# Remainders of streamed weights in a two-layer encoder trunk: an accumulating DMA onto the negated rounded part in place of a subtraction on VectorE

## Chip, cores and metric

One core of one Trainium2 chip runs the whole program. The metric is the device time of one execution in microseconds (us): 2113.9 us is the median of three runs before the change (2113.85 to 2116.01).

## The reference

The program computes a two-layer encoder trunk in float32 for one sequence of 512 tokens and 1024 features. Each layer has a SwiGLU feed-forward at half weight, a mixer, a second feed-forward, each followed by a layer norm over a scaled residual, and a gated per-layer embedding. Cut to its frame:

```python
def swiglu(x, wg, wu, wd):
    return (jax.nn.silu(x @ wg) * (x @ wu)) @ wd

def reference(x, p, ...):
    for i in range(DEPTH):
        x = layer_norm(DN_ALPHA * x + 0.5 * swiglu(x, ffn1_wg[i], ffn1_wu[i], ffn1_wd[i]), ...)
        y = mixer_ab(x, ...) if i % 2 == 0 else mixer_c(x, ...)
        x = layer_norm(DN_ALPHA * x + y, ...)
        x = layer_norm(DN_ALPHA * x + 0.5 * swiglu(x, ffn2_wg[i], ffn2_wu[i], ffn2_wd[i]), ...)
        x = x + jax.nn.sigmoid(x @ ple_wg[i] + ple_bg[i]) * (p[i] @ ple_wp[i])
    return x
```

The mixer of layer 0 is sliding-window attention beside a gated linear recurrence (mixer A and B), that of layer 1 a gated delta rule with eight heads (mixer C). The feed-forward width is 2816, so the four feed-forwards hold most of the weights.

## The kernel before

Activations lie with features on the partitions and the 512 tokens along the free axis. The weights are cut into 2776 tiles of 128x128, which the host packs in the order of their use; each tile is read from memory once.

**Products.** A float32 product is made of three passes in a rounded format (float32r). Both operands are split into a rounded part (hi) and the exact remainder (lo), and `mm3` (L338) issues lo x hi, hi x hi and hi x lo into one sum. The pass with the remainder of the weights comes first.

**The weight stream.** `dma_unit` (L293) loads a unit of eight tiles (512 KB) on SP's DMA queue into one of three buffers called wr. `splitter` (L299) splits the units by halves: a half unit is four tiles, 128x512 elements, and feeds twelve products. It allocates two tiles of the big pool (the t tiles, 93 buffers). ScalarE copies the half unit into hi with rounding, VectorE subtracts hi from the half unit and writes lo (L314 and L315):

```python
yield self.S.l.copy(hi[:, c].bitcast(F32R), r[:, c])
yield self.V.l.tensor_tensor(lo[:, c].bitcast(F32R), r[:, c], hi[:, c], ALU.subtract)
```

There are 694 half units. `splitter` runs ahead of the products by `self.ahead` half units: 4 in a feed-forward, 10 towards the end of a feed-forward or a mixer, 6 otherwise.

**The order of the work.** The program is written out by hand for each engine; each engine executes its instructions in that order and waits on semaphores. The main stream is TensorE's. All else is in chains (generators), and between two products `tick` (L233) lets each chain go on as far as its operands are there by a rough clock which the program keeps for every engine while it is built. The rough clock decides only the order.

**A feed-forward** (`ffn`, L401): eleven groups of four sums (two gate and two up tiles), each group eight half units of weights, 96 products. After a group ScalarE and VectorE read the sums from PSUM, and ScalarE goes on with the next splits. Then come the products with the third matrix, one sum after the other (`resid_ln`, L424). A feed-forward has 132 half units.

**The tail of a block** (`resid_ln`, L424, `tail`, L498): the sums of a layer norm are taken tile by tile. For the middle tiles POOL adds the values and their squares (8 to 12 additions of 128x512), for the last ones VectorE does it, and all of them build up the same two tiles; TensorE then sums over the partitions by products with a tile of ones (o), and the next block's inputs follow from that. In the two mixers three output tiles are made by halves of the tokens.

All compute instructions are issued by the helper `issue` at L100, so the profile puts nearly all of them on that line.

Of the kernel before, what the change touches and what calls it, by code (L numbers as in the profile page):

```python
"""Two-layer hybrid encoder trunk (macaron SwiGLU, sliding-window attention + RG-LRU,
gated DeltaNet, per-layer embeddings) on one NeuronCore.

Activations are feature-major ([feature on partitions, 512 tokens free]); every weight
matrix is streamed once, packed by the host in the order of its use, 128x128 tile by tile.
A float32 product is carried by three float32r passes: both operands are split exactly
into a rounded part and its remainder.
The delta rule runs in blocks of 128 tokens: v_new = beta * T (v - e^gc (k S)) with
T = (I + (strict kk^T decay) diag(beta))^-1, built by recursive block doubling.
"""  # L10
# [8 lines left out]
F32R = mybir.dt.float32r  # L19
AF = mybir.ActivationFunctionType  # L20
ALU = mybir.AluOpType
AX = mybir.AxisListType

P = 128
T = 512
# [17 lines left out]
# columns of the packed per-partition vectors  # L43
# [14 lines left out]
# columns of the constant table: identity, ones, cumulative-sum triangle, causal mask,  # L58
# compact identity, masks of the block-doubling levels
# [16 lines left out]
def cells(ap):  # L76
    """the 128-element columns of its tile that an access touches"""
    name = ap.tensor.name
    dims = list(ap.ap)
    c0 = ap.offset % dims[0][0]  # L80
    c1 = c0 + sum((n - 1) * st for st, n in dims[1:])
    return [(name, c) for c in range(c0 // P, c1 // P + 1)]


class Eng:
    """Issues to an engine and keeps a rough clock of it, by which the order of issue of
    independent work is chosen. eng.f(...) issues, eng.l.f(...) makes an Op to be issued later."""
# [25 lines left out]
    def at(self, op):  # L113
        """when the operands are there"""
        ready = self.k.ready
        return max([ready.get(c, 0.0) for x in op.ins for c in cells(x)] + [0.0])
# [44 lines left out]
class Kern:  # L161
# [44 lines left out]
    def bank(self, keep=2):  # L206
        """for chains: a PSUM bank, when more than keep are left for the main stream"""
        while len(self.banks) <= keep:
            yield None
        return self.take_bank()  # L210
# [9 lines left out]
    # The main stream is the tensor engine's, slot by slot. Chains are generators of Ops (or lists  # L220
    # of Ops of one engine); between the main stream's products each chain goes on as far as its
    # operands are there by the rough clock. None: look again later.
# [10 lines left out]
    def tick(self, share=None):  # L233
        """share: the time that chains may take on the tensor engine now"""
        if self.ticking:
            return False
        if share is not None:
            self.share = min(self.share + share, MAXSHARE)
        self.ticking = True
        moved = False  # L240
        for g in list(self.gens):
            n = 0
            while n < 12:
                n += 1
                op = g[1]
                if op is not None:
                    ops = op if isinstance(op, list) else [op]
                    if self.due_at(op) > self.PE.t or share is not None and ops[0].eng is self.PE and self.share <= 0.0:
                        break
                    t = self.PE.t  # L250
                    for o in ops:
                        o.eng.issue(o)
                    self.share -= self.PE.t - t
                    moved = True
                try:
                    g[1] = next(g[0])
                except StopIteration:
                    self.gens.remove(g)
                    moved = True
                    break  # L260
                if g[1] is None:
                    break
        self.ticking = False
        return moved
# [9 lines left out]
    def until(self, cond):  # L274
        """hold the main stream until the chains have issued what it needs"""
        n = 0
        while not cond():
            if not self.tick():
                at = [self.due_at(g[1]) for g in self.gens if g[1] is not None]
                self.PE.t = max(self.PE.t + 0.02, min(at) if at else 0.0)  # L280
            n += 1
            assert n < 100000

    def settle(self, *aps):
        """chains go on while the main stream's next operands are not there"""
        at = max([self.ready.get(c, 0.0) for x in aps for c in cells(x)] + [0.0])
        while at > self.PE.t + 0.05:
            if not self.tick():
                nxt = [self.due_at(g[1]) for g in self.gens if g[1] is not None]
                self.PE.t = max(self.PE.t + 0.02, min([at] + nxt))  # L290

# [7 lines left out]
    def splitter(self):  # L299
        """splits the weights some half units ahead of their use"""  # L300
        while self.nsplit < 2 * NUNITS:
# [9 lines left out]
            for c0, c1 in FIRST if v == 0 else ((0, HSLOT),):  # L311
                if c1 <= HSLOT:
                    c = slice(c0 * P, c1 * P)
                    yield self.S.l.copy(hi[:, c].bitcast(F32R), r[:, c])  # L314
                    yield self.V.l.tensor_tensor(lo[:, c].bitcast(F32R), r[:, c], hi[:, c], ALU.subtract)  # L315
                    self.units[v] = (hi, lo)
            self.nsplit += 1

    def w(self, desc):
        """the next weight tile of the stream, as its two parts"""  # L320
        u, s = divmod(self.nslot, HSLOT)
        if s == 0:
            # the splitter goes first when it is late
# [31 lines left out]
    def split(self, src, eng=None):  # L355
        """hi = rounded src, lo = src - hi; src in SBUF or PSUM"""
# [8 lines left out]
    def group(self, descs, x, nk=KD, halves=False):  # L365
        """the m tiles of a group advance together over k; with halves, tokens 0-255 first"""
# [20 lines left out]
    def x(self, k, cs):  # L387
        """layer input k, once its normalisation is issued"""
        half = 0 if cs.stop == T // 2 else 1
        self.until(lambda: self.napply[half] > k)  # L390
        return self.xh[k], self.xl[k]
# [32 lines left out]
    def resid_ln(self, i, l, fac, desc, y, nk, ngroup, nhalf):  # L424
        """x = LN(alpha x + fac y); y comes as 8 PSUM tiles: the first ngroup advance together
        over k, the last nhalf are made by halves of the tokens, so that the normalisation of the
        first half runs under the products of the second. Sums are taken about the mean of the
        first 128 features."""
# [55 lines left out]
        for half, cs in enumerate(HALVES):  # L484
            for m in ms:
                # a bank is not written while it is read
# [67 lines left out]
    def ple_p(self, i, ms):  # L554
        """products of p, made where the main stream would wait for a normalisation"""
# [13 lines left out]
    def ple(self, i):  # L569
# [26 lines left out]
        if last:  # L596
            # the last one by halves of the tokens, each on its way out under the other
# [19 lines left out]
    def softplus(self, x, n):  # L617
        """max(x,0) + log1p(exp(-|x|)), log1p by 2 atanh(e/(2+e))"""
# [74 lines left out]
    def attn(self, j, hh, q):  # L693
        """one head, two pairs of 128-query blocks; keys of the block and of the one before"""
# [59 lines left out]
    def conv(self, p_, cols, bias=None):  # L754
        """causal depthwise convolution over the free axis, taps w[0..3] per partition"""
# [24 lines left out]
    def rg_lru(self, t, x, pa, px):  # L780
        """with Th = tanh(-log_a / 2): y = 1/(1 + Th) by a Newton step from (1 + a)/2,
        a = 1 - 2 Th y, sqrt(1 - a^2) = 2 sqrt(Th) y"""
# [115 lines left out]
    def gdn(self, h):  # L898
# [9 lines left out]
        # decay: dt[j, i] = exp(gc_i - gc_j), j <= i  # L908
# [3 lines left out]
        # token-major k, q (for the norms) and v  # L912
# [37 lines left out]
        # U = (I + N)^-1, 32x32 diagonal blocks first (compact), then 64 and 128  # L950
# [15 lines left out]
        # level s: with the 2s blocks [lo | hi], the product of U11 N12 with U22 makes U12; two  # L966
        # chunks share a pass, the hi (then the lo) columns of both being 32
# [52 lines left out]
        # scan over the blocks  # L1020
# [149 lines left out]
# tiles of the pool; delta-rule chains at a time; heads by which a gate z follows its q, k, v  # L1170
# [3 lines left out]
# products of p made before the second feed-forward, and before the gates  # L1174
NP1, NP2 = 5, 8
# half units split ahead at the end of a feed-forward, of a mixer
AHEADF, AHEADO = 10, 10
# chains on the tensor engine: lateness allowed for operands, time per main product, bursts
PELAG, SHARE, MAXSHARE = 0.15, 0.25, 0.2
LOOK = 2  # L1180
AB_ORDER = (("bx", 1), ("q", 1), ("g", 0), ("bx", 2), ("q", 2), ("g", 1), ("bx", 3), ("q", 3), ("g", 2),
# [3 lines left out]
def c_order():  # L1185
    """the q, k, v of a head ahead of the gate z of an earlier one"""
# [26 lines left out]
def alibi():  # L1213
    """[head, query, own | previous | own keys], relative to a block of 128 queries"""
# [83 lines left out]
```

## Time and profile before

| | before |
|---|---|
| median of 3 runs | 2113.9 us (2113.85 to 2116.01) |
| span of the profiled execution | 2113.2 us |
| TensorE (PE) busy | 2093.3 us, 99% |
| TensorE weight loads (PEld) busy | 1757.3 us, 83% |
| VectorE (DVE) busy | 1102.8 us, 52% |
| ScalarE (ACT) busy | 867.1 us, 41% |
| GpSimd (POOL) busy | 145.5 us, 7% |
| DMA | 194.38 MB, mean 92 GB/s |
| mean granted TensorE clock | 0.998 |

The profiled execution is another one than the timed runs. Its own time is its span, 2113.2 us from the first to the last instruction; the runs' times hold 0.7 us more at the median. Busy shares are means over stages which differ: the four feed-forwards, the two mixers and the layer norms between them. TensorE's bounds stand out at once; where it does wait, and for whom, is in the views by time. Matmul ends are modelled, so the sum of busy time alone does not show a stall.

### The profile page before, as it was taken

Reading aid. Unit: us, or ns where it says so; the run is one execution under the profiler, and the core shown is the slowest. Engines: PE = TensorE matmul, PEld = TensorE weight load, DVE = VectorE, ACT = ScalarE, POOL = GpSimd, SP = SyncE. Lnnn points to the kernel's source line nnn. Section 1 sums busy time; section 2 is a strip of 40 time slices with the busy share of each in tenths; the row PEclk is TensorE's granted clock in tenths of the full one; section 3 lists DMA queues with packets and bytes.
Section 4 is the critical chain, followed back from the end, with each engine's and each line's share of the span. In section 5 each row is a group of like instructions: output and inputs, shape, how many; then the busy total and the mean of one; then the engine's idle time right before and its main releaser. Section 6 shows DMA issues by size and latency. Waiting matters only on the chain. (4 is left out here: it accounts for less than half of the span.)

```text
span 2113.2 us, 29415 instructions
## 1 busy us (share of the span) xinstructions
PE 2093.3 (99%) x11773; PEld 1757.3 (83%) x11773; DVE 1102.8 (52%) x2146; ACT 867.1 (41%) x1795; POOL 145.5 (7%) x120
## 2 busy tenths in 40 slices
PE   9999999999999999999999999999999999999999
PEld 7888888878888888898888888977777898888888
DVE  5334345778833334484333344867776763343456
ACT  4323224665623322263323223674754452232244
POOL 0000012001100001100000011020210200000110
PEclk9999999999999999999999999999999999999999
DMA  5323234113232323313232324132221213232331
GB/s 180 118 81 105 85 110 150 41 52 99 79 102 81 119 80 101 133 56 110 90 109 80 110 87 143 33 85 65 51 63 59 90 62 119 80 113 78 108 120 51
DMA packets 55754, 194.38 MB, mean 92 GB/s; under 512 B 6320, under 2 KB 7232, under 8 KB 55616
## 3 DMA queue, kind: packets, MB, share of 16 engines
q1 hardware_dynamic: 54432, 188.81, 27.6%
q0 software_dynamic: 1184, 3.69, 0.9%
q8 instruction: 92, 1.51, 0.3%
q14 instruction: 46, 0.38, 0.1%
HBM read 190.35 MB, written 2.11 MB: 91 GB/s over the span
## 5 line engine op out<-in xcount | busy, mean ns | idle before, releaser
L100 PE MATMUL ps<-t,t 128*128 128x512 f32 (+5 forms) x10640 | 2049.8, 354 | 7.1 <-ACT t L100 4.3
L100 PEld LDWEIGHTS ps<-t,t 128*128 128x128 f32 (+3 forms) x10640 | 1692.4, 184 | 319.2 <-issue 17.8
L100 DVE TENSOR_TENSOR t<-wr,t 128x512 fp32r<-128x512 f32 (+1 forms) x695 | 485.7, 741 | 163.7 <-ACT t L100 159.3
L100 ACT CAST t<-wr 128x512 fp32r<-128x512 f32 (+1 forms) x695 | 393.8, 616 | 193.2 <-DMA wr<-w 192.9
L100 DVE TENSOR_TENSOR t<-t,ps 128x512 f32<-128x512 f32 (+1 forms) x126 | 71.1, 565 | 440.3 <-PE ps L100 251.9
L100 ACT ACTIVATE t<-ps 128x512 f32<-128x512 f32 (+2 forms) x172 | 78.9, 462 | 501.6 <-PE ps L100 501.3
L100 DVE TENSOR_TENSOR t<-t,t 128x512 fp32r<-128x512 f32 (+3 forms) x314 | 176.0, 571 | 62.6 <-ACT t L100 56.1
L100 POOL TENSOR_TENSOR t<-t,t 128x512 f32<-128x512 f32 x64 | 98.3, 1555 | 1601.8 <-DVE t L100 1581.9
L100 ACT CAST t<-t 128x512 fp32r<-128x512 f32 (+1 forms) x253 | 130.0, 518 | 162.7 <-DVE t L100 160.0
L100 ACT ACTIVATE t<-t 128x512 f32<-128x512 f32 (+1 forms) x118 | 66.4, 572 | 260.6 <-DVE t L100 256.6
L100 DVE SCALAR_TENSOR_TENSOR t<-ps,t 128x512 f32<-128x512 f32 (+2 forms) x74 | 43.9, 600 | 212.5 <-PE ps L100 212.5
L100 DVE SCALAR_TENSOR_TENSOR t<-ps,vec,t 128x511 f32<-128x511 f32 (+3 forms) x92 | 68.2, 743 | 21.1 <-ACT t L100 17.4
L100 ACT ACTIVATE t<-t,vec,der 128x256 f32<-128x256 f32 x96 | 55.2, 597 | 5.8 <-DVE t L100 5.8
L100 ACT ACT_TABLE_LOAD x37 | 47.5, 1283 | 10.7 <-DVE t L100 9.5
L100 DVE SCALAR_TENSOR_TENSOR t<-t,t 128x512 f32<-128x512 f32 (+2 forms) x64 | 38.2, 605 | 21.0 <-ACT t L100 19.7
L100 DVE SCALAR_TENSOR_TENSOR t<-t,der,t 128x256 f32<-128x256 f32 x96 | 45.8, 477 | 0.0
L100 ACT COPY t<-ps 128x512 f32<-128x512 f32 (+1 forms) x59 | 33.0, 567 | 28.1 <-PE ps L100 27.9
L100 PEld LDWEIGHTS ps<-cst,t 128*128 128x128 f32 (+1 forms) x300 | 35.4, 148 | 10.8 <-issue 2.3
L100 PE MATMUL ps<-cst,t 128*128 128x128 f32 (+2 forms) x300 | 41.5, 261 | 1.4 <-DVE t L100 1.4
L100 DVE TENSOR_TENSOR t<-t 128x256 f32<-128x256 f32 x96 | 40.1, 420 | 2.6
L100 POOL TENSOR_TENSOR y<-y,sm 128x8 f32<-128x8 f32 (+1 forms) x16 | 22.9, 1434 | 190.0 <-DVE y L100 189.9
L100 ACT ACTIVATE t<-ps,vec 128x512 f32<-128x512 f32 x28 | 19.4, 699 | 23.8 <-PE ps L100 23.8
(66 smaller groups left out, 412.8 us busy)
## 6 DMA issues: line engine op xcount, KB each, us to landing
wr<-w SPq DMA_DIRECT2D x346, 512.0 KB, 4.2
t<-x SPq DMA_DIRECT2D x8, 256.0 KB, 6.3
t<-p SPq DMA_DIRECT2D x8, 256.0 KB, 5.0
t<-gcd POOLq DMA_DIRECT2D x8, 256.0 KB, 5.3
out<-t SPq DMA_DIRECT2D x7, 256.0 KB, 2.0
t<-bias POOLq DMA_DIRECT2D x8, 192.0 KB, 3.7
cst<-cst SPq DMA_DIRECT2D x1, 352.0 KB, 5.8
wr<-w SPq DMA_DIRECT2D x2, 128.0 KB, 2.9
```

Source lines behind the costliest of these rows:

```text
L100: getattr(self.e, op.name)(*op.a, **op.kw)
```

## The change

From half unit 4 on (`NDIRECT`), VectorE's subtraction is replaced by two steps. ScalarE writes the negated, rounded half unit into lo (an activation Copy with scale -1.0), which makes lo = -hi. Then a DMA on POOL's queue reads the same half unit of the weights from memory again and adds it into lo where it lies: lo = w - hi. The rough clock takes lo as there 5.0 us after the DMA's issue (`LOADD`). The first four half units keep the subtraction. The copy into hi, the loads of the units and the products stay.

```diff
                     yield self.S.l.copy(hi[:, c].bitcast(F32R), r[:, c])
-                    yield self.V.l.tensor_tensor(lo[:, c].bitcast(F32R), r[:, c], hi[:, c], ALU.subtract)
+                    if v < NDIRECT:
+                        yield self.V.l.tensor_tensor(lo[:, c].bitcast(F32R), r[:, c], hi[:, c], ALU.subtract)
+                    else:
+
+                        yield self.S.l.activation(lo[:, c].bitcast(F32R), r[:, c], AF.Copy, scale=-1.0)
+                        c0 = (v % 2) * HSLOT * P
+                        self.nc.gpsimd.dma_start(lo.bitcast(F32R), self.a["w"][v // 2, :, c0:c0 + HSLOT * P],
+                                                 accum_op=ALU.add)
+                        for x in cells(lo):
+                            self.ready[x] = max(self.S.t, self.PE.t) + LOADD
                     self.units[v] = (hi, lo)
...
+NDIRECT, LOADD = 4, 5.0
```

The rest of the diff drops comments. In the instruction order VectorE has 2118 rows before and 1433 after, ScalarE 1624 and 2309, POOL 125 and 815, TensorE 9789 in both. Two places are spoken of below.

ScalarE at the start of the program, from the split of half unit 4 on. CAST is the copy with rounding, wr is a buffer of loaded weights, t_84 to t_87 are activations x, the other t tiles are hi and lo. Before:

```order
L100 CAST t_182<-t_84 128x512 [waits DMAHW0_49]
L100 CAST t_177<-wr_102 128x512 [waits DMAHW1_49]
L100 CAST t_200<-wr_102 128x512
L100 CAST t_189<-t_85 128x512 [waits DMAHW2_49]
L100 CAST t_208<-wr_146 128x512 [waits DMAHW0_49]
L100 CAST t_215<-t_86 128x512 [waits DMAHW3_49]
L100 CAST t_222<-wr_146 128x512
```

and after the change:

```order
L100 CAST t_182<-t_84 128x512 [waits DMAHW0_49]
L100 CAST t_177<-wr_102 128x512 [waits DMAHW1_49]
L100 ACTIVATE t_178<-wr_102 128x512
L100 CAST t_199<-wr_102 128x512
L100 ACTIVATE t_200<-wr_102 128x512
L100 CAST t_189<-t_85 128x512 [waits DMAHW2_49]
L100 CAST t_211<-wr_146 128x512 [waits DMAHW0_49]
L100 CAST t_222<-t_86 128x512 [waits DMAHW3_49]
L100 ACTIVATE t_212<-wr_146 128x512
```

Behind each rounding of a half unit stands its negation; the DMA that waits for it is the next row on POOL's queue.

POOL at the tail of mixer A and B, where it adds up the values and the squares of four tiles (t_4427 and t_4426 before, t_4602 and t_4601 after). Before:

```order
L100 TENSOR_TENSOR t_4427<-t_80,t_81 128x512 [waits DVE_49,PE_49,Activation_49]
L100 TENSOR_TENSOR t_4426<-t_4426,t_4465 128x512 [waits Activation_49]
L100 TENSOR_TENSOR t_4427<-t_4427,t_82 128x512 [waits DVE_49,Pool_49]
L100 TENSOR_TENSOR t_4426<-t_4426,t_4473 128x512 [waits Activation_49,Pool_49]
L100 TENSOR_TENSOR t_4427<-t_4427,t_83 128x512 [waits DVE_49]
L100 TENSOR_TENSOR t_4426<-t_4426,t_4482 128x512 [waits DVE_49,Activation_49]
L100 TENSOR_TENSOR t_4427<-t_4427,t_84 128x512 [waits DVE_49]
L100 TENSOR_TENSOR t_4426<-t_4426,t_4492 128x512 [waits DVE_49,Activation_49]
```

and after the change:

```order
L100 TENSOR_TENSOR t_4601<-t_4601,t_4658 128x512 [waits Activation_49]
L321 DMA t_4647<-w 128x512 [waits DMASW2_49,Activation_49]
L100 TENSOR_TENSOR t_4601<-t_4601,t_4665 128x512 [waits Pool_49]
L321 DMA t_4716<-w 128x512 [waits DMASW3_49,PE_49,Activation_49]
L100 TENSOR_TENSOR t_4602<-t_4602,t_83 128x512 [waits DVE_49]
L321 DMA t_4733<-w 128x512 [waits DMASW4_49,Activation_49]
L100 TENSOR_TENSOR t_4601<-t_4601,t_4673 128x512 [waits DVE_49,Pool_49]
L321 DMA t_4758<-w 128x512 [waits DMASW5_49,Activation_49]
L100 TENSOR_TENSOR t_4602<-t_4602,t_84 128x512 [waits DVE_49]
L321 DMA t_4776<-w 128x512 [waits DMASW6_49,Activation_49]
L100 TENSOR_TENSOR t_4601<-t_4601,t_4682 128x512 [waits DVE_49]
```

The first two additions stand ahead of the rows shown. Five DMA issues now stand among the eight additions, each with a wait for ScalarE.

## Rows read from the trace of the kernel before

**Rows 1.** The page: span, and busy time, share and instructions by engine.
```profile
span 2113.2 us, 29415 instructions
PE 2093.3 (99%) x11773; PEld 1757.3 (83%) x11773; DVE 1102.8 (52%) x2146; ACT 867.1 (41%) x1795; POOL 145.5 (7%) x120
```

**Rows 2.** Groups by line and form: count | busy us, mean ns | idle before, releaser.
```profile
L100 DVE TENSOR_TENSOR t<-wr,t 128x512 fp32r<-128x512 f32 x693 | 484.8, 741 | 163.5 <-ACT t L100 159.1 <-issue 4.0
L100 ACT CAST t<-wr 128x512 fp32r<-128x512 f32 x693 | 393.0, 616 | 190.8 <-DMA wr<-w 190.6
L100 ACT ACTIVATE t<-t 128x512 f32<-128x512 f32 x86 | 53.3, 630 | 233.4 <-DVE t L100 229.7 <-DVE y L100 2.4 <-DVE s L100 1.1
L910 POOL DMA_DIRECT2D t<-gcd x8 | 6.4, 796 | 1.8 <-DMA gcd<-t 1.8
L642 POOL DMA_DIRECT2D t<-bias x8 | 4.5, 564 | 5.8 <-PE ps L100 5.8
```

**Rows 3.** ScalarE's timeline in a feed-forward: start us, us, instructions, idle before, releaser.
```profile
95.72 2.70 ACT L100 CAST t<-wr 128x512 fp32r<-128x512 f32 x5
100.66 1.14 ACT L100 CAST t<-wr 128x512 fp32r<-128x512 f32 x2 [2.23 <-DMA wr<-w]
103.13 0.62 ACT L100 CAST t<-wr 128x512 fp32r<-128x512 f32 x1 [1.32 <-DMA wr<-w]
113.57 0.60 ACT L100 ACTIVATE t<-ps 128x512 f32<-128x512 f32 x1 [9.82 <-PE ps L100]
...
117.48 2.70 ACT L100 CAST t<-wr 128x512 fp32r<-128x512 f32 x5
```

**Rows 4.** Busy time by stretch, with granted clock, DMA share, GB/s; ScalarE's roundings 1380:1420.
```profile
14.00:16.00 2.00, 2.00 (x10) 1.65 (x9) 0.67 (x2) 0.00 (x0) 0.00 (x0) 1.00 1.04 416
50.00:246.00 196.00, 196.00 (x867) 162.29 (x866) 69.29 (x109) 60.54 (x109) 0.00 (x0) 1.00 0.30 97
1380.00:1420.00 40.00, 38.85 (x286) 31.70 (x285) 27.50 (x63) 33.01 (x91) 13.26 (x13) 1.00 0.30 76
L100 ACT CAST t<-wr 128x512 fp32r<-128x512 f32 x11 | 6.8, 622 | 0.0
```

**Rows 5.** DMA issues on the page: count, KB each, median us to landing.
```profile
t<-x SPq DMA_DIRECT2D x8, 256.0 KB, 6.3
t<-bias POOLq DMA_DIRECT2D x8, 192.0 KB, 3.7
```

**Rows 6.** DMA queue of POOL from 361 to 372 us: packets, MB, share of 16 engines.
```profile
q0 software_dynamic: 512, 1.57, 42.7%
```

**Rows 7.** ScalarE's timeline at the start of the program.
```profile
12.12 1.14 ACT L100 CAST t<-wr 128x512 fp32r<-128x512 f32 x2 [0.36 <-DMA wr<-w]
16.77 0.62 ACT L100 CAST t<-wr 128x512 fp32r<-128x512 f32 x1 [2.99 <-DMA wr<-w]
26.47 0.60 ACT L100 ACTIVATE t<-ps 128x512 f32<-128x512 f32 x1 [0.44 <-PE ps L100]
```

**Rows 8.** Subtractions 514:540; POOL's additions (min/median/max ns); POOL's first and last there.
```profile
L100 DVE TENSOR_TENSOR t<-wr,t 128x512 fp32r<-128x512 f32 x11 | 11.1, 1021 | 0.0
L100 POOL TENSOR_TENSOR t<-t,t 128x512 f32<-128x512 f32 x8 | 12.2, 1538 | 158.2 <-DVE t L100 158.2
L100 POOL TENSOR_TENSOR t<-t,t x64: 1263/1640/1779, 277.4 to 2043.0; 128x512 f32<-128x512 f32 x64
521.72 5.96 POOL L100 TENSOR_TENSOR t<-t,t 128x512 f32<-128x512 f32 x4 [155.99 <-DVE t L100]
534.82 1.27 POOL L100 TENSOR_TENSOR t<-t,t 128x512 f32<-128x512 f32 x1 [0.42 <-DVE t L100]
```

**Rows 9.** TensorE's timeline at the tails of the two mixers.
```profile
537.52 0.39 PE L100 MATMUL ps<-t,o 128*128 128x256 f32 x1 [3.40 <-ACT t L100]
1680.90 0.39 PE L100 MATMUL ps<-t,o 128*128 128x256 f32 x1 [3.29 <-ACT t L100]
```

## The prediction, made before the changed kernel had run

> **What bounds the kernel now.** I read the page's shares first, then the groups by line, then one group of a feed-forward in ScalarE's timeline, then the busy time by stretches, and last the places where TensorE waits. TensorE is busy 2093.3 of 2113.2 us, VectorE 1102.8, ScalarE 867.1 [rows 1]: the reader is to see that less work on VectorE is worth nothing by itself, and that TensorE's 19.9 us without work are all there is to win. The groups by line show what is exchanged: 693 subtractions of 741 ns that make the remainders, 484.8 us, and beside them the 693 roundings on ScalarE [rows 2].
>
> The timeline shows the rhythm. In a feed-forward ScalarE rounds eight half units (four weight tiles, twelve products each) in a burst, then waits for the sums of the group. Bursts start at 95.72 and 117.48, so a group of eight takes 21.76 us and a half unit 2.72 us [rows 3]. The first sum of group 4 is read at 113.57; that is its last half unit with one tile of four done, so the group ends three tiles later, at about 113.5 + 3 x 0.68 = 115.5, and began at 93.8. The burst at 95.72 opens with half unit 37, the sixth of that group, which TensorE reaches at 93.8 + 5 x 2.72 = 107.4. **The lead is 11.7 us.** In that stage the DMA engines are busy 0.30 of the time [rows 4].
>
> The sum is made on the profiled execution's 2113.2 us. The median of the runs is 2113.9; the 0.7 between them is carried along unchanged.
>
> **The subtractions.** 690 of them leave VectorE (the four first half units keep theirs). At 741 ns that is 511 us of an engine that TensorE does not wait for in the feed-forwards: 0 us there. The two places where it can matter are taken below.
>
> **The negations.** ScalarE gets 690 activations of 128x512 from SBUF. The nearest row has 630 ns [rows 2], so 435 us, and ScalarE goes from 867 to about 1302 of 2113 us. In a burst a half unit costs it 1.25 instead of 0.62 us, 10 us for eight; after 95.72 there are 17.9 us until the next sums, so even with the 3.5 us or so that it waits for loads it is done in time: 0 us. Where it is fullest, 33.0 of 40 us [rows 4], the eleven roundings of that stretch bring 6.9 us more, which fills it; TensorE already idles 1.15 us there. I take 0 and keep +2 us as the upper end.
>
> **The accumulating DMAs: latency.** 690 DMAs of 256 KB go out on POOL's queue. The nearest row for issue and landing is the table of biases, 192 KB by the same queue: 564 ns per issue, landing 3.7 us after it [rows 2, 5]. From the start of the rounding to the landing that is 1.25 + 3.7 = 5 us, and with the 6.3 us of an activation load in the crowded start [rows 5] 7.6 us. Both lie under the lead of 11.7 us: 0 us, as long as the DMA engines keep up.
>
> **The accumulating DMAs: throughput.** This is the term that decides. A group needs 8 x 8 = 64 rows of 2 KB on each of the 16 engines. The loads take 0.30 x 21.76 = 6.5 us of a group, so 15.2 us are left, 238 ns for one row. The trace has no accumulating DMA. A plain row is bounded by three rows: at 97 GB/s and a share of 0.30 an engine moves 20.2 GB/s, 2 KB in 101 ns; at 416 GB/s with all engines busy 26 GB/s, 79 ns [rows 4]; POOL's own queue took 0.427 x 11 us x 16 / 512 = 147 ns for packets of 3 KB, 98 ns for 2 KB [rows 6]. An accumulation reads the weights and the negated part, and writes: the lower end is one plain row, 79 ns, where all of it overlaps; the upper end is three in a row, 303 ns. I take two, 200 ns, since in a plain copy the read and the write already lie in the one duration, and only a second read comes on top. That makes 12.8 + 6.5 = 19.3 of 21.76 us, 89% of the engines: it fits, and costs **0 us**. At three rows it is 19.4 + 6.5 = 25.9 us, and the stage is bound by the DMA engines (rival B). The Trainium skill, in "Collectives: The Full Stack", section "The bandwidth ceiling: the fold count and why AG ≠ RS ≠ AR", says that an add inside the DMA engine costs no cycles and that only its second source read counts, with a measured ratio of 1.93 to a copy. By that rule the row is some 195 ns and the sum stays as it is; no run here has shown it yet.
>
> **The start.** The first accumulated half unit is number 4. Group 0's first sum is read at 26.47, so its last half unit ends at 28.5, and half unit 4 starts 4 x 2.72 earlier, at 17.6. ScalarE rounds numbers 4 and 5 from 12.12 to 13.26 [rows 7]; with the negation behind its rounding number 4 is ready to issue at 13.3. With the landing of the bias table it is there at 17.0, in time; but at 14 to 16 us the DMA engines are full [rows 4], and the activation loads of the same 256 KB took 6.3 us in that crowd: 19.6, which is 2.0 us late. With a second read of 1.6 us on top it is 21.2, 3.6 us late. I take **+2.0 us**, with 0 and 3.6 as ends. Number 6, whose load arrives at 16.77, is ready to issue at 18.6 when the engines are free again, and lands about when the shifted TensorE wants it.
>
> **The tails of the two mixers.** Here VectorE is without a gap, and in 514 to 540 us eleven subtractions take 11.1 us of it, stretched to 1021 ns by POOL's additions beside them [rows 8]. TensorE waits 3.40 us at 537.52 and 3.29 us at 1680.90 for what follows from these sums [rows 9]. All of it, 6.7 us, would be won if VectorE set the end. But the eight additions of sums and squares on POOL run from 521.72 to 536.09 [rows 8], and the wait on TensorE ends right behind them. In the changed order five DMA issues stand among these eight additions, each behind its negation on ScalarE. Eight times 1538 ns and five times 564 to 796 ns are 15.1 to 16.3 us against the 14.4 of now: 0.7 to 1.9 us lost per tail. If the additions fall to the 1263 ns of their shortest, with VectorE quieter beside them, it is 12.9 us and 1.5 us are won. I take 0 for both, with -3.0 and +3.8 as ends. Late next here is POOL.
>
> **The sum.** 2113.2 + 0.7 + 2.0 + 0 + 0 = **2115.9 us**. Its own range, from the ends of the terms, is 2113.9 - 3.0 = 2110.9 to 2113.9 + 3.6 + 3.8 + 2 = 2123.3. About 0.2%, 4.2 us, is what a measurement of this kernel can tell from no change: 2109.7 to 2118.1 counts as the same.
>
> **The rivals.**
> B, slower: the DMA engines become the bound. Place: the four feed-forwards, 132 half units each, 66 groups. It decides from 238 ns a row on; at 255 ns a group takes 6.5 + 16.3 = 22.8 us, 1.06 more than now and +70 us over 66 groups, 2186; at 303 ns it is 4.1 us more and +273 us, 2389. For it: the headroom is only 11%, and POOL's packets are no faster than SP's. Against it: the same engines moved 416 GB/s at the start, where a row took 79 ns, and two of those are 158.
> C, faster: the tails are won back. VectorE's eleven subtractions are gone there and the sums come earlier. 2115.9 - 6.7 = 2109.2, or 2107.2 without a loss at the start. For it: VectorE is full for 25 us at both places. Against it: POOL's chain, above.
> D, slower: an accumulation lands later than the lead of 11.7 us although the engines keep up, because POOL issues it late or its reads queue behind loads. Each us too many is paid once a group, 66 us: 2182 for the first. Against it: 5 to 7.6 us leave 4 us to spare.
> That VectorE keeps the subtractions is excluded by the changed order, where 690 DMAs stand on POOL's queue.
>
> **How the numbers follow.** The forecast's case has 0.64: all three bounds of a plain row (101, 79 and 98 ns) lie under 238 ns when taken twice. B has 0.21, since a quarter or so of the span from 79 to 303 ns lies above 238. C has 0.11, D 0.04. (By the Trainium skill's rule on the second source read, in the page and section named above, B would have less than half of its chance.) Faster by over 0.2%: 0.06 of C and 0.03 of the forecast's case, 0.09. Slower: B, D and 0.15 of the forecast's case, whose upper end lies above 2118.1, 0.40. The same: the rest, 0.51. The range goes from 2108 to 2190: it leaves out the lowest part of C (0.04) and those parts of B and D that lie above 2190 (0.14).
>
> **What would show it.** The DMA share in a group of the first feed-forward: about 0.9 and bursts every 21.76 us if the forecast holds, near 1.0 and bursts further apart if B does. The accumulating DMAs' landing: 5 to 8 us; above 11.7 us is D. TensorE's wait before half unit 4, near 17.6 us: about 2 us. TensorE's waits at the tails: about 3 us still, under 1 us if C holds, and POOL without gaps between its additions there. VectorE busy some 600 us, ScalarE some 1300. The prediction is wrong if the feed-forward's groups stretch, or if waits for accumulations appear outside the start.

## The result, and the profile after

The changed kernel takes 2129.4 us (median of 4, 2126.4 to 2138.8), the kernel before 2114.2 us on the same chip. The ratio is 1.0075, its 95% interval 1.0063 to 1.0088: slower by 15.2 us. That is inside the range given (2108 to 2190), but above the forecast's own range, which ended at 2123.3, and none of the rivals describes it. The execution that was profiled is the longest of the four, so the trace below shows some 9 us more than the median, and its mean granted clock is 0.991 where the three others have 0.994 to 0.995; where that matters the text says so.

The first lines of the page, against [rows 1]:

```profile
span 2137.0 us, 30910 instructions
PE 2106.7 (99%) x11773; PEld 1766.9 (83%) x11773; DVE 652.3 (31%) x1456; ACT 1218.9 (57%) x2485; POOL 728.2 (34%) x810
```

VectorE lost 450 us of busy time and ScalarE gained 352, where 511 and 435 were reckoned from durations: the records of neighbouring instructions overlap (five roundings of 0.62 us take 2.70 us in [rows 3]), so an engine's busy time changes by less than their sum. The groups by line (count | busy us, mean ns | idle before, releaser) show where it went:

```profile
L321 POOL DMA_DIRECT2D t<-w x690 | 609.9, 943 | 1214.9 <-ACT t L100 1016.7 <-PE ps L100 97.2 <-issue 55.5
L100 ACT ACTIVATE t<-wr 128x512 fp32r<-128x512 f32 x690 | 435.0, 630 | 3.2 <-PE ps L100 3.2
```

The negation is what [rows 2] said, 630 ns. The issue is not: 943 ns against the 564 of the bias table, and POOL, which was nearly idle, now spends 610 us on issuing.

**The feed-forwards hold.** Busy time from 50 to 250 us (columns as in [rows 4]), and then the DMA queues and landings of the same stretch (packets, MB, share of 16 engines; count, KB each, median us to landing):

```profile
50.00:250.00 200.00, 200.00 (x884) 165.58 (x884) 24.39 (x37) 97.33 (x180) 62.29 (x72) 1.00 0.85 194
```

```profile
q0 software_dynamic: 10723, 19.53, 55.8%
...
t<-w POOLq DMA_DIRECT2D x72, 256.0 KB, 10.1
```

TensorE is busy 200.00 of 200 us at a granted clock of 1.00, the DMA engines 0.85 of the time. 72 accumulations are 72 x 128 = 9216 rows of 2 KB; 0.558 x 200 x 16 / 9216 = 194 ns for one. The bursts on ScalarE are still 21.76 us apart (at 102.06 and 123.82 us). The median landing of 10.1 us is above the 5 to 8 us that were forecast; what it leaves of the lead is taken up behind the experiments.

**Where the time went.** The products with the matrix of ones mark the ends of the stages in TensorE's timeline (start us, us, count), in the kernel before and then in the changed one:

```profile
362.02 0.39 PE L100 MATMUL ps<-t,o 128*128 128x256 f32 x2
...
550.21 0.40 PE L100 MATMUL ps<-t,o 128*128 128x256 f32 x2
...
1328.28 0.39 PE L100 MATMUL ps<-t,o 128*128 128x256 f32 x2
...
1693.67 0.40 PE L100 MATMUL ps<-t,o 128*128 128x256 f32 x2
...
2052.06 0.43 PE L100 MATMUL ps<-t,o 128*128 128x256 f32 x2
```

```profile
367.76 0.39 PE L100 MATMUL ps<-t,o 128*128 128x256 f32 x2
...
558.13 0.40 PE L100 MATMUL ps<-t,o 128*128 128x256 f32 x2
...
1336.68 0.40 PE L100 MATMUL ps<-t,o 128*128 128x256 f32 x2
...
1716.04 0.40 PE L100 MATMUL ps<-t,o 128*128 128x256 f32 x2
...
2074.29 0.39 PE L100 MATMUL ps<-t,o 128*128 128x256 f32 x2
```

The differences between neighbours, here and in two of the experiments told below, are a ledger (us; each column adds up to its span):

| stretch | before | after | start mended (e1) | all three mended (e10) |
|---|---|---|---|---|
| start and first feed-forward | 362.0 | 367.8 | 361.2 | 361.5 |
| first mixer with its tail | 188.2 | 190.4 | 189.7 | 183.2 |
| second and third feed-forward | 778.1 | 778.6 | 778.7 | 779.1 |
| second mixer with its tail | 365.4 | 379.4 | 369.1 | 358.3 |
| fourth feed-forward | 358.4 | 358.3 | 358.3 | 358.7 |
| to the end | 61.1 | 62.7 | 62.5 | 62.3 |

The second, third and fourth feed-forward lose less than half a microsecond together. The loss is in the start and in the mixers. Three places in TensorE's timeline (idle time and releaser in brackets) show it:

```profile
22.26 247.82 PE L100 MATMUL ps<-t,t 128*128 128x512 f32 x1086 [4.12 <-DMA t<-w]
...
542.69 0.38 PE L100 MATMUL ps<-t,o 128*128 128x256 f32 x1 [3.00 <-ACT t L100]
544.67 0.58 PE L100 MATMUL ps<-t,o 128*128 128x256 f32 x1 [1.60 <-DVE t L100]
...
1401.89 1.08 PE L100 MATMUL ps<-cst,t 128*128 128x128 f32 x4 [5.20 <-DVE t L100]
```

*The start.* TensorE waits 4.12 us for the first accumulation. POOL began to issue it at 14.15, so it landed some 8 us later.

*The decay table.* At 1401.89 TensorE waits 5.20 us for a chain of the second mixer; before, the wait at this place was 1.15 us. VectorE had waited for the read-back of the decay table (`t<-gcd`, the eight issues in [rows 2]). TensorE before, then VectorE in the changed kernel:

```profile
1396.77 0.66 PE L100 MATMUL ps<-cst,t 128*128 128x128 f32 x4 [1.15 <-DVE t L100]
```

```profile
1397.70 0.69 DVE L100 TENSOR_TENSOR t<-t,cst 128x512 f32<-128x512 f32 x1 [4.75 <-DMA t<-gcd]
```

POOL's timeline, of the kernel before and then of the changed one:

```profile
1383.94 0.51 POOL L892 DMA_DIRECT2D gcd<-t  x1 [72.09 <-DVE t L100]
1386.25 2.29 POOL L910 DMA_DIRECT2D t<-gcd  x3 [1.80 <-DMA gcd<-t]
```

```profile
1386.30 0.87 POOL L321 DMA_DIRECT2D t<-w  x1 [5.71 <-ACT t L100]
1386.84 0.86 POOL L901 DMA_DIRECT2D gcd<-t  x1
1391.51 1.58 POOL L919 DMA_DIRECT2D t<-gcd  x2 [3.81 <-issue]
```

Before, POOL had issued nothing for 72 us, the table's write landed after 1.7 us, and the read-back went out 2.3 us behind it. Now an accumulation stands directly ahead of the write, which lands after 3.4 us, and the read-back goes out 4.7 us behind it.

*The tails.* [rows 8, 9] showed POOL's eight additions and TensorE's waits of 3.40 and 3.29 us. POOL's timeline at the first tail now:

```profile
533.46 0.88 POOL L321 DMA_DIRECT2D t<-w  x1 [1.32 <-ACT t L100]
534.06 1.60 POOL L100 TENSOR_TENSOR t<-t,t 128x512 f32<-128x512 f32 x1
535.30 1.20 POOL L321 DMA_DIRECT2D t<-w  x1
535.91 1.92 POOL L100 TENSOR_TENSOR t<-t,t 128x512 f32<-128x512 f32 x1
...
541.86 1.18 POOL L321 DMA_DIRECT2D t<-w  x1
542.47 1.86 POOL L100 TENSOR_TENSOR t<-t,t 128x512 f32<-128x512 f32 x1
```

Issues and additions take turns; the chain ends at 544.3 and TensorE at 544.67 behind it. VectorE, whose subtractions are gone, now has gaps there (busy 23.57 of 35 us from 520 to 555 us, 33.18 before), but TensorE's waits are 4.60 us where they were 3.79 (3.40 and 0.39).

*The clock.* Behind these waits the granted clock is lower: the first row below is the stretch after the wait for the decay table. The two others have no wait of TensorE in them, only a lower clock (0.47 and 0.21 of 10 us missing, 6.8 us by estimate). The traces of e1 and e3 do not have this: from 1520 to 1560 us their clock is 1.00.

```profile
1400.00:1410.00 10.00, 8.11 (x29) 6.72 (x30) 2.79 (x4) 4.12 (x10) 3.09 (x4) 0.66 0.22 41
1530.00:1540.00 10.00, 10.00 (x67) 6.66 (x66) 4.70 (x12) 2.72 (x7) 2.30 (x2) 0.53 0.22 62
1540.00:1550.00 10.00, 10.00 (x80) 7.90 (x79) 5.17 (x14) 3.64 (x8) 2.12 (x3) 0.79 0.33 54
```

### The profile page after: what moved, and what is told of

It reads as the page before. It is cut to its first block, busy times and chain, and to the rows that moved or that the text cites. A ratio compares the mean times of both kernels' runs of the same rounds, so it can differ in the third digit from the quotient of the medians.

```text
span 2137.0 us, 30910 instructions
## 1 busy us (share of the span) xinstructions
PE 2106.7 (99%) x11773; PEld 1766.9 (83%) x11773; DVE 652.3 (31%) x1456; ACT 1218.9 (57%) x2485; POOL 728.2 (34%) x810
## 5 line engine op out<-in xcount | busy, mean ns | idle before, releaser
L100 PEld LDWEIGHTS ps<-t,t 128*128 128x128 f32 (+2 forms) x10640 | 1701.5, 185 | 325.3 <-issue 19.7
L321 POOL DMA_DIRECT2D t<-w x690 | 609.9, 943 | 1214.9 <-ACT t L100 1016.7
L100 ACT CAST t<-wr 128x512 fp32r<-128x512 f32 (+1 forms) x695 | 424.9, 612 | 168.4 <-DMA wr<-w 159.5
L100 ACT ACTIVATE t<-wr 128x512 fp32r<-128x512 f32 x690 | 435.0, 630 | 3.2 <-PE ps L100 3.2
L100 DVE TENSOR_TENSOR t<-t,t 128x512 fp32r<-128x512 f32 (+3 forms) x314 | 181.2, 591 | 118.7 <-ACT t L100 106.3
L100 POOL TENSOR_TENSOR t<-t,t 128x512 f32<-128x512 f32 x64 | 90.0, 1413 | 115.0 <-DVE t L100 114.4
L100 ACT ACT_TABLE_LOAD x37 | 47.5, 1283 | 11.6 <-DVE t L100 10.4
L100 ACT ACTIVATE t<-ps,der 128x512 f32<-128x512 f32 (+2 forms) x26 | 16.2, 657 | 29.0 <-PE ps L100 29.0
```

What stands on the lines that cost most here:

```text
L100: getattr(self.e, op.name)(*op.a, **op.kw)
L321: self.nc.gpsimd.dma_start(lo.bitcast(F32R), self.a["w"][v // 2, :, c0:c0 + HSLOT * P], accum_op=ALU.add)
```

## The experiments

The theory after the trace: the first accumulations, the decay table behind them on POOL's queue, and POOL's chain in the tails are the loss. Rivals: the 435 us on ScalarE, or the 181 MB of additional traffic as such. Each kernel was timed beside the kernel before on its chip; ratios are against that, and differences in us are between the two medians.

**e1, the start alone.**
```diff
-NDIRECT, LOADD = 4, 5.0
+NDIRECT, LOADD = 12, 5.0
```


> The changed kernel with twelve first half units subtracted on VectorE instead of four. Theory: the loss at the start is the late landing of the first accumulations alone (TensorE waits 4.12 us at 22.26 and then runs at a lower granted clock; the first ones-products come 5.7 us later than before). Then the wait goes, the landmark is back near 362 us, and the time falls by 5 to 6 us, to about 2124. Rival: half unit 12 is just as late as half unit 4 was, since the crowd of loads only moves the wait; then the gain is under 1 us, 2128 to 2130.

2121.0 us, ratio 1.0038 (1.0025 to 1.0052), +5.8 us: by the ratio about half of the loss is gone. TensorE's timeline has no wait from 8.89 us to the end of the first feed-forward:

```profile
8.89 254.66 PE L100 MATMUL ps<-t,t 128*128 128x512 f32 x1122 [0.27 <-DVE t L100]
```

The first stretch of the ledger falls by 6.6 us. The theory said 5 to 6, and 2124; the rival, that half unit 12 is just as late, falls.

**e2, the feed-forwards alone.**
```diff
-                    if v < NDIRECT:
+                    if v < NDIRECT or (132 <= v < 192 or 462 <= v < 556):
...
-NDIRECT, LOADD = 4, 5.0
+NDIRECT, LOADD = 12, 5.0
```


> Accumulations only in the four feed-forwards and their surroundings: the first twelve half units and all of the two mixers (half units 132 to 191 and 462 to 555) keep the subtraction. Theory: the start and the mixers hold all of the loss, the feed-forwards none; the time is that of the kernel before, 2113 to 2117. Rival: the feed-forwards carry a share of the loss that the profiled execution hides (a lower clock, late accumulations here and there); then 2120 or more.

2116.0 us, ratio 1.0007 (0.9998 to 1.0015): as expected, not to be told from the kernel before. 528 accumulations, in the feed-forwards and what borders on them, cost nothing that can be measured, and give nothing either.

**e3, the second mixer alone.**
```diff
-                    if v < NDIRECT:
+                    if not 462 <= v < 556:
```


> Accumulations only in the second mixer (half units 462 to 555), the subtraction everywhere else. Theory: most of the loss arises here, +7 to +14 us over the kernel before, 2121 to 2128, with a wait of TensorE behind the DMA of the decay table. Rival: the loss needs the whole stream of accumulations behind it (queues that have run full), or was a matter of one execution; then +0 to +4, 2114 to 2118.

2118.1 us, ratio 1.0011 (1.0002 to 1.0019): +2.9 us, below what was expected of the theory. The wait is there, though, with a queue that carried no accumulations before this mixer:

```profile
1391.00 1.02 PE L100 MATMUL ps<-cst,t 128*128 128x128 f32 x4 [3.44 <-DVE t L100]
```

What the profiled execution of the changed kernel lost more in this mixer (14.0 against 3.5 us) is thus not the accumulations' place alone: its wait was 1.8 us longer and its clock lower.

**e4, ScalarE's share.** The DMA and the landing behind it are replaced by an addition on VectorE.
```diff
-                        self.nc.gpsimd.dma_start(lo.bitcast(F32R), self.a["w"][v // 2, :, c0:c0 + HSLOT * P],
-                                                 accum_op=ALU.add)
...
+                        yield self.V.l.tensor_tensor(lo[:, c].bitcast(F32R), lo[:, c], r[:, c], ALU.add)
```


> The negations on ScalarE stay, the DMAs go: VectorE adds the weights to the negated rounded part (as many operations on VectorE as in the kernel before, 690 more on ScalarE than there). If ScalarE's 435 us are what costs in the mixers: +7 to +15 us over the kernel before, 2121 to 2129. If the accumulating DMAs and POOL's queue are: +0 to +3, 2114 to 2117.

2116.2 us, ratio 1.0012 (1.0003 to 1.0021): +1.0 us by the medians, 2.5 by the ratio, as expected if the DMAs and POOL's queue are what costs. ScalarE's 435 us cost little by themselves; as the cause of 15 us they are out.

**e5, the decay table on another queue.** e3 with one edit more, in both places:
```diff
-        self.nc.gpsimd.dma_start(gd, gt[0:32, 0:P])
+        self.nc.sync.dma_start(gd, gt[0:32, 0:P])
...
-        self.nc.gpsimd.dma_start(b3(egb), self.gcd.rearrange("(c h) t -> h c t", c=NB)[h:h + 1].to_broadcast([P, NB, P]))
+        self.nc.sync.dma_start(b3(egb), self.gcd.rearrange("(c h) t -> h c t", c=NB)[h:h + 1].to_broadcast([P, NB, P]))
```


> Accumulations only in the second mixer, as in the run before it, but the nine DMAs of the decay table (one write, eight reads back) go out on SP's queue instead of POOL's. Theory: the decay table is late because it stands behind accumulations on POOL's queue (landing 3.4 us instead of 1.7 us). Then the wait of TensorE behind it, 3.44 us there, falls to about 1 us, the second mixer is some 2 us shorter, and the time goes back to 2113 to 2116. Rival: the wait comes from the order of the products (only 4 products of the main stream stand ahead of the chain's product where 13 stood before), whatever queue the table takes; then the wait stays above 2.5 us and the time at 2117 to 2119.

2114.4 us, ratio 1.0000 (0.9991 to 1.0008). At the place where TensorE waited 3.44 us it goes on without a gap, since the table is there in time (SP's timeline, then TensorE's):

```profile
1378.34 0.34 SPq L901 DMA_DIRECT2D gcd<-t  x1
1379.83 0.94 SPq L919 DMA_DIRECT2D t<-gcd  x2
```

```profile
1388.30 0.60 PE L100 MATMUL ps<-cst,t 128*128 128x128 f32 x4
```

The order of the products is that of e3, so the rival falls: it was the queue. The write lands after 1.4 us and the read-back goes out 1.5 us behind it, where it was 3.4 and 3.7 us in e3 (1377.70 to 1381.43). The Trainium skill, in "DMA: Bandwidth & Descriptors", section "SWDGE vs HWDGE vs iDMA", says that only one queue is allocated for the DMAs that GpSimd issues, and that those of SP go to other queues inside each DMA engine, served in turn. This pair of runs agrees.

**e6 and e7, the tails.** e6 is the kernel before with the two mixers' sums on VectorE:
```diff
-            self.spawn(first(p_) if m == 0 else take(m, p_, FULL, True, G), 1)
+            self.spawn(first(p_) if m == 0 else take(m, p_, FULL, True, V), 1)
...
-            self.spawn(take(m, self.mtile(desc(m), y, nk), FULL, True, G), 1)
+            self.spawn(take(m, self.mtile(desc(m), y, nk), FULL, True, V if nk == KD else G), 1)
```


> The kernel before, subtractions and all, with one edit: the sums and sums of squares of the two mixers' normalisations are added on VectorE instead of POOL. Control for the next run. VectorE has no gap in the tails and gets eight operations of about 0.68 us more in each, 5.4 us; without POOL beside it the stretched operations there (up to 1.5 us for a subtraction of 0.68) get shorter by some 4 us. So -1 to +2 us per tail, 2112 to 2119.

2112.7 us, ratio 0.9990 (0.9981 to 0.9999): 2.3 us faster, within what was expected. TensorE now waits for VectorE, at the first tail 1.59 us and at the second 0.97:

```profile
538.97 3.96 PE L100 MATMUL ps<-t,t 128*128 128x256 f32 x20 [1.59 <-DVE t L100]
```

e7 has the same edit in the changed kernel, where only the half units of the tails accumulate:
```diff
-                    if v < NDIRECT:
+                    if not (174 <= v < 192 or 538 <= v < 556):
```


> Accumulations only for the half units that are split in the tails of the two mixers (174 to 191 and 538 to 555), and the sums added on VectorE. If the chain on POOL (eight additions with DMA issues between them) is what held the tails in the changed kernel: VectorE now has room for them, TensorE's waits at both places fall from 3.4 + 0.4 and 3.3 + 0.5 us to under 1 us each, and the time is 2108 to 2111. Rival: the tail is bound by its own chain of dependent operations; the waits stay at 2 us or more and the time is within 2 us of the kernel before.

2105.8 us, ratio 0.9957 (0.9945 to 0.9970): faster than the kernel before by 9.3 us, below the 2108 to 2111 that were expected; the rival falls. The places of [rows 9] in TensorE's timeline:

```profile
535.35 0.85 PE L100 MATMUL ps<-t,o 128*128 128x256 f32 x2 [0.70 <-ACT t L100]
...
1673.23 0.84 PE L100 MATMUL ps<-t,o 128*128 128x256 f32 x2
```

Waits of 7.5 us (3.40 and 3.29, and 0.39 and 0.45 for the products behind them) are down to 0.70, and the two mixers' stretches of the ledger to 183.0 and 358.9 us, 5.2 and 6.5 less than before. VectorE's eight additions at the first tail, by line and form from 510 to 545 us, take less than half of the 12.2 us that POOL took for them [rows 8]:

```profile
L100 DVE TENSOR_TENSOR t<-t,t 128x512 f32<-128x512 f32 x8 | 5.1, 684 | 1.5 <-ACT t L100 1.4
```

**e8, twice the requests.** e2 with a second, plain DMA behind each accumulation, whose data nobody reads, and four tiles less in the big pool:
```diff
+                        sc = self.scr.tile([P, HSLOT * P], F32, tag="scr", name=self.name("sc"))
+                        self.nc.gpsimd.dma_start(sc, self.a["w"][v // 2, :, c0:c0 + HSLOT * P])
```


> Accumulations only in the feed-forwards, and with each of them a plain DMA of the same 256 KB of weights into a buffer that nobody reads (four such buffers, paid for by four tiles less in the big pool). It doubles the requests on POOL's queue. Theory of the break-even: a group of 21.76 us has 15.2 us for them, 238 ns for a row and its accumulation; 190 ns of the accumulation and 80 to 150 ns of the plain row make 270 to 340 ns, so the feed-forwards become bound by the DMA engines: a group takes 24 to 28 us, the time is 2115 plus 66 x 2 to 6.5 us, 2250 to 2540, with DMA shares of 0.97 or more there. Rival: the engines overlap the rows of different requests and share of busy time is no limit; then the time stays under 2150.

2159.3 us in two runs, ratio 1.0209 (1.0191 to 1.0228): between the two, and neither as told. From 50 to 250 us the queue's share rises, and TensorE still does not wait (the row from 100 to 200 us behind it):

```profile
q0 software_dynamic: 16515, 38.65, 79.1%
...
t<-w POOLq DMA_DIRECT2D x73, 256.0 KB, 9.1
```

```profile
100.00:200.00 100.00, 100.00 (x443) 82.81 (x442) 10.68 (x16) 47.72 (x88) 52.55 (x74) 1.00 1.06 291
```

A row and its accumulation take 0.791 x 200 x 16 / (73 x 128) = 271 ns, over the 238 of the break-even, and the group does not stretch at once: the busy share goes to 1.06, so packets of different queues overlap. The waits for weights begin at 339.5 us, late in the first feed-forward. In the whole trace TensorE waits only 11.2 us for accumulations; the largest waits, 9.22 us below and one of 10.68, stand in the normalisations behind feed-forwards, where ScalarE in turn waited for POOL (6.59 us before 922.27), which issues, adds, and waits for the four buffers:

```profile
926.05 1.04 PE L100 MATMUL ps<-t,o 128*128 128x256 f32 x2 [9.22 <-ACT t L100]
```

So the break-even is soft: past it the lead is eaten up first, and the price comes late and elsewhere. e8 doubles POOL's issues too, so its 44 us are not a price of the DMA engines alone.

**e9, the tails with POOL's chain.** e7 without the edit of the sums.

> Accumulations only for the half units split in the tails of the two mixers (174 to 191 and 538 to 555), the sums still added on POOL. It separates the two edits of the kernel that ran at 2105.8 us. If POOL's chain is what holds the tails: eight additions with five or more issues between them take as long as the eight additions beside VectorE's subtractions did, TensorE's waits stay near 3 us each (3.4 + 0.4 and 3.3 + 0.5 before, 1.3 + 1.6 where accumulations ran in the second mixer), and the time is 2113 to 2117. Rival: VectorE's subtractions alone were the cause, and the additions' place is a detail; then 2106 to 2110.

2116.1 us, ratio 1.0006 (0.9997 to 1.0015), as expected. TensorE's waits are 3.25 and 1.62 us at the first tail, and 1.20 and 1.60 at the second, where about 3 had been expected:

```profile
536.86 0.38 PE L100 MATMUL ps<-t,o 128*128 128x256 f32 x1 [3.25 <-ACT t L100]
538.86 0.58 PE L100 MATMUL ps<-t,o 128*128 128x256 f32 x1 [1.62 <-DVE t L100]
```

Accumulating in place of VectorE's subtractions wins nothing alone, taking POOL's additions away alone wins 2.3 us, both together 9.3: whichever of the two is relieved, the other holds the tail. e9 also puts DMA issues among POOL's additions; what the additions alone would hold with the subtractions gone, no run shows.

**e10, the whole change with three edits.** The changed kernel with the edits of e1, e5 and e6.

> The whole change with its three costs mended: twelve first half units subtracted on VectorE, the decay table's DMAs on SP's queue, the sums of the mixers' normalisations added on VectorE; all other half units accumulate. If the start, the decay table and POOL's chain are all of the loss, the tails' gain of some 9 us shows here too, less the 1 to 3 us that 690 negations on ScalarE cost: 2106 to 2110. Rival: 690 accumulations cost something more (the mixers' traffic, late landings there, the clock); then 2112 or more.

2104.8 us, ratio 0.9951 (0.9937 to 0.9964): 10.2 us faster than the kernel before, and below what was expected. 682 half units still accumulate. The page and TensorE's timeline at the second tail:

```profile
span 2103.1 us, 30919 instructions
PE 2091.0 (99%) x11773; PEld 1755.4 (83%) x11773; DVE 655.2 (31%) x1480; ACT 1212.2 (58%) x2477; POOL 699.5 (33%) x777
```

```profile
1672.61 0.39 PE L100 MATMUL ps<-t,o 128*128 128x256 f32 x2
```

Neither traffic nor ScalarE keeps the gain back. e7 reaches nearly the same with 36 accumulations, the intervals overlap: the gain is in the tails alone.

## Why the prediction was right or wrong

**The subtractions and the negations: right in size.** Taking 354 us of busy time from VectorE, nearly all in the feed-forwards, is worth nothing (e2: 749.2 against 1102.8). The negations cost nothing in the feed-forwards; alone they cost 1.0 us by the medians and 2.5 by the ratio (e4, interval 0.6 to 4.4), about the +2 us that was kept as an end. In a burst a half unit takes ScalarE 1.05 us, not 1.25, for the overlap told above (102.06 to 103.11).

**Throughput: right, by its own steps.** 200 ns were taken for a row, 194 measured; a share of 0.89 was expected, 0.85 came, and the groups did not stretch. The rule cited from the Trainium skill, in "Collectives: The Full Stack", section "The bandwidth ceiling: the fold count and why AG ≠ RS ≠ AR", gave an estimate of some 195 ns (1.93 times 101); its ratio was measured on collectives, and the trace agrees with 194. What was too sharp is rival B's price: at the 271 ns of e8 a group would take 6.5 + 17.3 = 23.8 us, and 66 groups 137 us more; e8 paid 44.

**Latency: wrong in size, without a price in the feed-forwards.** 3.7 to 6.3 us were taken for the landing, from a bias table and an activation load that have no such burst beside them; in bursts of eight on one queue the median is 10.1 us. It is not the first of a burst that lands so late. In the burst from 102.06 us the seven issues from 103.50 to 109.76 land after 5.3, 8.0, 9.6, 11.2, 11.6, 12.3 and 12.0 us. By the prediction's own reckoning TensorE reaches the first of them at 113.7 us and each further one 2.72 us later, while the issues are 1.04 us apart. So the first has 4.9 us to spare and the next three about 4, an estimate from these rows: the 4 us that spoke against rival D were there, since the lead grows along the burst as the landings do.

**The start: the mechanism was right, the term was mis-sized.** +2.0 us was taken between 0 and 3.6. The landing took some 8 us, past the 6.3 us of the activation load by about the second read's 1.6, and half unit 4 was issued 0.9 us later than reckoned (14.15 for 13.3). The wait is 4.12 us; with 0.5 us of another wait (for a subtraction on VectorE, at 9.69) and a lower clock behind them the stretch is 5.7 us longer. Of three rows for the landing the one in the same crowd, with its upper end, was the nearest; the middle was taken.

**A term that was missing: what else stands on POOL's queue.** The step on latency priced 690 DMAs by whether they arrive in time for TensorE, and named nobody behind them. The eight read-backs of the decay table stood in [rows 2] with 1.8 us of idle time before them, spent on the landing of its write. That they would now follow accumulations, which no wait in the program shows, was to be had from the order of POOL's instructions. e3 and e5 price it: 3.6 us in the second mixer's stretch of the trace (368.8 against 365.3), 3.5 us in the medians, each taken against the kernel before on its own chip (the intervals of the two ratios overlap a little).

**The tails: right, including what is late next.** 0 was forecast because POOL's chain of additions would be the next bound, with issues in between. The trace shows that chain, the waits changed by +0.8 and +0.1 us, and e9 and e7 show that rival C's gain was real and only held back by it. TensorE's clock was no term of the sum, and it belongs to both: over the 35 us from 520 it was 0.95 before and 0.90 in the changed kernel, 1.75 us more, which with the 0.8 us of waits is about what the first mixer lost. C's 6.7 us were too low: 9.3 came. The second products' waits add 0.8, and over 35 us at each tail (from 520 and from 1655 us) the clock rose from 0.95 to 1.00 in e7 and e10, 1.75 us in each. So TensorE's 19.9 us without work were not quite all there was to win.

**The verdict.** "The same" had 0.51 and slower 0.40; slower came, 13.5 us above the 2115.9 that were forecast. The time lies in the stated range only because that range was stretched to 2190 for rivals B and D, and neither of them happened; that it holds the time is luck. Of the signs named, waits for accumulations outside the start did not come: TensorE's only wait for one is at the start. What came is a wait behind one, the decay table's, which no sign named.

**What stays open.** The stretch after the last feed-forward is 1.2 to 1.6 us longer in e1, e2, e10 and the changed kernel, and not in e3, where no accumulations run there; no run took it apart. In e7's trace, too, the stretches outside the mixers are together 2.1 us longer than before. The lower clock from 1530 to 1550 us is told, not explained; two of e1's six times, 2128.0 and 2129.3 us, also come with a mean clock of 0.992 where the four others have 0.996 or 0.997, and have no trace.

## What to carry to other kernels

Work that is moved to a queue is not only early or late by itself: list what else goes out on that queue, and price what now stands behind it. When an engine is relieved and nothing gets faster, look at the engine it takes turns with; here the gain appeared only when both VectorE's subtractions and POOL's additions were out of the tail, and additions on the path do not go well on a POOL that issues DMAs between them. Let the first users of a stream that starts late keep the old way: twelve instead of four half units gave back about half of the loss.

## What the runs showed that was not expected

An accumulating DMA of 256 KB costs POOL 943 ns to issue on average, 860 to 870 ns where nothing runs beside it and up to 1.57 us between additions (e3's second tail). A plain one of the same size is cheaper: the shortest issue in e8 is 0.56 us for the plain DMAs and 0.85 for the accumulating ones.

VectorE's subtraction of 128x512 takes 1021 ns beside POOL's additions [rows 8]; in e6, from 510 to 545 us and with POOL idle, it takes 685 ns, and the additions that moved to VectorE 680. So the kernel got faster by moving 5.4 us of work onto an engine without a gap, since that engine's other operations got shorter:

```profile
L100 DVE TENSOR_TENSOR t<-wr,t 128x512 fp32r<-128x512 f32 x15 | 9.6, 685 | 1.9 <-ACT t L100 1.9
```

The Trainium skill, in "SBUF — State Buffer", section "Who interferes with whom", says that an operation of VectorE on two tensors in SBUF contends with what GpSimd reads; the two numbers agree.

The DMA engines' busy share can pass 1: 1.06 over 100 us in e8, at 291 GB/s, where 0.85 was 194 GB/s. A share near 0.9 was not the edge that the forecast took it for, and the 1.04 in [rows 4] could have said so.
